# Inverting the scan's triangular blocks on TensorE by doubling, in a one-core RWKV-7 layer

## The chip, the cores and the metric

The kernel runs on one core of a Trainium2 chip. The metric is the device time in microseconds (us) of one execution of the whole program. Engines are written as in the profile: PE is TensorE (PEld its weight loads), DVE is VectorE, ACT is ScalarE, POOL is GpSimd, and SP is the engine whose queue issues the DMAs.

## The reference, cut to what matters

One inference step of a transformer-like layer: a SwiGLU feed-forward block, a token mixer, a second feed-forward block, on 128 context tokens and 1024 latent tokens with 1024 channels. The change is inside the token mixer, whose scan is the recurrence below, for 8 heads of size 64 and in both directions.

```
def step(S, inp):
    r_t, w_t, k_t, v_t, kk_t, a_t = inp
    sa = jnp.einsum('bhij,bhj->bhi', S, -kk_t)
    S = (S * w_t[:, :, None, :]
         + sa[..., None] * (kk_t * a_t)[:, :, None, :]
         + v_t[..., None] * k_t[:, :, None, :])
    return S, jnp.einsum('bhij,bhj->bhi', S, r_t)
```

The kernel computes the recurrence by chunks of 64 tokens. Inside a chunk, the vectors `sa` of the 64 tokens depend on each other through a strictly triangular 64x64 matrix N, so that the chunk needs the inverse of the unit triangular matrix I - N. A chunk's inverse does not depend on the state; only its use does.

## The kernel before

The program has three phases: feed-forward 1, the token mixer, feed-forward 2. In the mixer, the scan is cut into 18 items (`items`): two groups of four heads times eight pairs of chunks, and two context items. An item covers two chunks of four heads in each direction: 16 triangular 64x64 matrices with 32 diagonal 32x32 blocks. A direction's tile has 128 partitions (two heads, two blocks of 32 rows) and 4 matrices side by side.

For each item, three pieces of code run:

- `front` calls `stage_b` once per direction. It loads `ops` (a single buffer, 768 KB) from DRAM, makes decays and scaled operands on DVE and ACT (`fl`, `bk`, `e`), forms the raw matrices on PE (`scr`), masks them on DVE into `TT` (tile `ab`), and transposes `bk` (`bkt`). Lines L960 to L1000.
- `solve` turns the triangular matrices in `TT` into their inverses. Lines L1018 to L1089. The diagonal 32x32 blocks are copied by ACT (L995), written to DRAM (`nd`, L996) and read back with one whole block per partition (`un`, L1023; each block on four partitions). There DVE substitutes row by row: a multiply (L1036) and a sum over the last axis (L1037) for each of 7 + 2 x 3 steps, 26 instructions. The result goes through DRAM again (`xdd`, four writes L1047, two reads L1055 and L1056) back to the 32x32 layout. PE transposes it (`trx`, 24 matmuls of 32x32, L1064 and L1069), and two products of 16 matmuls each (`l64`, `l64b`, L1079 and L1084) join two 32x32 inverses to one 64x64 inverse.
- `seq_latent` or `seq_ctx` calls `step` twice. It is the state-dependent chain, in four rounds of small matmuls (`sq`, `yp`, L1121 to L1142) with copies by ACT and DVE between them.

Beside the scan, PE works off `filler`: the dense projections of the mixer (`pj`, three matmuls of 128x384 for each block, L705 to L707), and side jobs (`stage_k`, `stage_v`, `finish`; tiles `cps`, `kkb`, `bon`, `vt`, `gm`, `gv`) that need their own DMAs. A scheduler sets the order on every engine from priorities and its own cost estimates: the scan chain has the highest priority (`chain`, offset 40000), the side jobs come next, and the filler takes the places left. Each engine then runs its order strictly in sequence, so one late operand holds up everything behind it. SP's queue is in order too.

All matmuls of the scan are in fp32; the trace shows two records for each of them (L1079 issues 16 per item and 18 items give 576 records).

Of the kernel before, what the change touches and what calls it, by code (L numbers as in the profile page):

```python
# [31 lines left out]
C_ID, C_BO, C_MF, C_MB, C_SM, C_SEL, C_ONE, C_E, C_N = 0, 128, 256, 384, 512, 772, 774, 776, 856  # L32


def constants():
    c = np.zeros((128, C_N), np.float32)
    c[:, C_ID:C_ID + 128] = np.eye(128)
    hd = np.arange(128) // 64
    c[:, C_BO:C_BO + 128] = hd[:, None] == hd[None, :]
    s = np.arange(64)  # L40
    for col, keep in ((C_MF, lambda a, b: (a < b, a <= b)), (C_MB, lambda a, b: (a > b, a >= b))):
        strict, incl = keep(s[:, None], s[None, :])
        m = np.concatenate([strict, incl], 1)
        c[:, col:col + 128] = np.concatenate([m, m], 0)
# [6 lines left out]
    unit = np.zeros((32, 4, 10, 8), np.float32)  # L51
    unit[:, :, :8] = np.eye(8)
    for rep in range(4):
        for cc in range(2):
            unit[:, rep, 8 + cc, 2 * rep + cc] = 1
    c[:, C_E:C_E + 80] = unit.reshape(128, 80)
    return c
# [3 lines left out]
def body(ctx: ExitStack, tc: tile.TileContext, I: dict, y_prompt, y_sample, new_state):  # L61
# [16 lines left out]
    def pd(name="pd"):  # L78
        """a PSUM bank for a dense product, in the phases without the scan"""
# [8 lines left out]
    # ---------------------------------------------------------------- constants  # L88
# [9 lines left out]
    unit = cst[:, C_E:C_E + 80]  # L98
# [37 lines left out]
    # ---------------------------------------------------------------- pieces  # L136
# [22 lines left out]
    class Beside:  # L159
        """small products, issued after the dense products traced so far"""  # L160
# [14 lines left out]
    class Later:  # L175
        """work beside the dense products, each piece of it so many of them after the one before"""
# [98 lines left out]
    def postnorm(t, O, ssum, gp, spill, want_sum, xpool, sp):  # L275
        """x += gate * rms(O), in place of O; with want_sum the scale of the next norm."""
# [102 lines left out]
    # ---------------------------------------------------------------- FFN  # L379
# [68 lines left out]
    # ================================================================ FFN 1  # L448
    with ExitStack() as ph:
# [4 lines left out]
        def x_third(t, xp, PE, gap):  # L454
            """a third of the tokens by channels, and the scale of its norm"""
# [123 lines left out]
    # ================================================================ token mixer  # L579
# [3 lines left out]
    # ================================================================ FFN 2  # L583
    with ExitStack() as ph:
# [7 lines left out]
        def rows_of(name, tag, src, k, eng):  # L592
            """a channel block of the last third by tokens"""
# [59 lines left out]
def mixer(nc, tc, pool, env):  # L653
# [7 lines left out]
    unit = e.unit  # L661
# [6 lines left out]
    # derived per-channel parameters  # L668
# [9 lines left out]
    # per half of the partitions: the factors of b~ and k~ in the order of its rows  # L678
# [16 lines left out]
    nd = [dram.tile([2, 16, 1024], F32, name=f"nd{i}") for i in range(NI)]  # L695
    xdd = [dram.tile([2, 16, 1024], F32, name=f"xdd{i}") for i in range(NI)]
# [23 lines left out]
    def mirrored(p, row, sign, t0, n):  # L720
        """a row of the operands of a pair, and for the second head the row after or before it"""
# [24 lines left out]
    with ExitStack() as ph:  # L746
# [8 lines left out]
        YS = st.tile([128, 256], F32, name="ys")  # L755
# [4 lines left out]
        for t_ in UB + [YS]:  # L760
            G.memset(t_, 0.0)
# [106 lines left out]
        def shifted(t, d):  # L868
            """(column, source token, count) of the tokens of a third that have a neighbour."""
# [57 lines left out]
        def stage_v(p, t0, n, zv):  # L927
            """V by tokens, of a pair of heads and a block of tokens"""
# [19 lines left out]
        def zi(g, b):  # L948
            """the place of V and of the outputs of a quarter of the latents"""
            return b if g == 0 else (1, 0, 3, 2)[b]  # L950

        def stage_b(g, d, t0, A, it):
            """operands of a direction for the two chunks of tokens t0.., of two pairs of heads"""
# [51 lines left out]
        def ap_(t_, off, dims):  # L1005
            return bass.AP(tensor=t_.tensor, offset=t_.offset + off, ap=[list(t_.ap[0])] + [list(x) for x in dims])

        def diag(t_, d, s0, nb):
            """the blocks of a direction, partition by partition of the rows of a chunk"""
            return bass.AP(tensor=t_.tensor, offset=t_.offset + (d * 16 + s0 * 4) * 1024, ap=[[32, 128], [4096, nb], [1, 32]])  # L1010

        def every4(t_, r, n):
            """the partitions 4 v + r of a tile, first n columns"""
            ps = t_.ap[0][0]
            return bass.AP(tensor=t_.tensor, offset=t_.offset + r * ps, ap=[[4 * ps, 32], [1, n]])

        def solve(A, it):
# [4 lines left out]
            un = sc.tile([128, 1152], F32, name="un", tag="un")  # L1022
            SP.dma_start(un[:, 0:1024], bass.AP(tensor=nd[it].tensor, offset=nd[it].offset, ap=[[1024, 32], [0, 4], [1, 1024]]))  # L1023
            Lm = sc.tile([128, 1024], F32, name="lm", tag="lm")
            V.tensor_copy(Lm[0:64].rearrange("p (i j) -> p j i", j=32), un[0:64, 0:1024].rearrange("p (a b) -> p a b", b=32))
            S.activation(out=Lm[64:128], in_=un[64:128, 0:1024], func=AF.Copy)
            V.memset(ap_(Lm, 0, [(33, 32)]), 1.0)
            X8 = sc.tile([128, 320], F32, name="x8", tag="x8")
            S.activation(out=X8.rearrange("p (b x) -> p b x", b=4), in_=unit.unsqueeze(1).to_broadcast([128, 4, 80]), func=AF.Copy)
            tb = sc.tile([128, 4, 4, 32], F32, name="tb", tag="tb")  # L1030
            RR = tb[:, 0].rearrange("p s c -> p (s c)")[:, 0:48]

            def dot(out, a, b, dims):
                n = int(np.prod(dims))
                pv = ap_(un, 0, [(n // int(np.prod(dims[:k + 1])), dims[k]) for k in range(3)])
                V.tensor_tensor(out=pv, in0=a, in1=b, op=ALU.mult)  # L1036
                V.tensor_reduce(out=out, in_=pv, axis=AX.X, op=ALU.add)  # L1037
# [3 lines left out]
            V.tensor_copy(ap_(YS, 0, [(72, 4), (32, 2), (1, 8)]), ap_(X8, 64, [(80, 4), (8, 2), (1, 8)]))  # L1041
            for B in range(1, 4):
                n, w = 2 * B, 8 * B
                dot(ap_(RR, 0, [(8, n), (1, 8)]), ap_(Lm, 32 * w, [(0, n), (32, 8), (1, w)]), ap_(YS, 0, [(32, n), (0, 8), (1, w)]), (n, 8, w))
                dot(ap_(YS, w, [(32, n), (1, 8)]), ap_(X8, 80 * B, [(0, n), (1, 8), (8, 8)]), ap_(RR, 0, [(8, n), (0, 8), (1, 8)]), (n, 8, 8))
            for r in range(4):
                SP.dma_start(xdd[it].rearrange("d u (b r x) -> (d u) b r x", b=4, r=4)[:, :, r],  # L1047
                                         every4(YS, r, 256).rearrange("p (b x) -> p b x", b=4))
            T0, T1 = A["T"]

            def blk(t_, h, r, c):
                return t_[quad(h, r), :, 32 * c:32 * c + 32]
# [422 lines left out]
```

## Time and profile before

| what | value |
|---|---|
| median of 3 runs | 3307.19 us (3301.38, 3307.19, 3314.62) |
| profiled execution, first to last instruction (span) | 3303.1 us |
| profiled execution, own time | 3314.62 us, 11.5 us around the span |
| PE busy | 3036.7 us, 92% |
| DVE busy | 1914.0 us, 58% |
| ACT busy | 1201.1 us, 36% |
| POOL busy | 395.3 us, 12% |

The profiled execution is taken to be the longest of the three runs, since its span is longer than the shortest run and some time lies around every span. Busy time is the union of an engine's instructions. The mixer's scan lies at about 1100 to 2215 us of the span; in the feed-forward phases before and behind it nearly every slice of PE is in its highest tenth. PEclk is the clock granted to TensorE as a share of 2.4 GHz; it takes only two values, 1.0 and 0.5, so a mean of 0.89 says that 22% of a stretch ran at 1.2 GHz.

### The profile page before, as it was taken

The numbers are of one execution on the slowest core, as the hardware profiler recorded it, in microseconds if no ns is written. First come the engines' busy times: TensorE is split into PE (matmuls) and PEld (weight loads), VectorE is DVE, ScalarE is ACT, GpSimd is POOL, SyncE is SP. The second block draws the span as 40 slices with busy tenths as digits, with TensorE's granted clock in tenths as the row PEclk, the third lists the DMA queues.
The fourth block names the chain that finished last, engine by engine and source line by source line (L and its number), as shares of the span: only waits on it lengthen the run. The fifth ranks groups of instructions, "written<-read, shape, count | busy, mean of one in ns | idle before, by whom it ended". The sixth has DMA issues, their size and how long they took to land.

```text
span 3303.1 us, 54285 instructions
## 1 busy us (share of the span) xinstructions
PE 3036.7 (92%) x20956; PEld 2850.3 (86%) x20956; DVE 1914.0 (58%) x4282; ACT 1201.1 (36%) x2726; POOL 395.3 (12%) x327
## 2 busy tenths in 40 slices
PE   8999999999989677788888889899989999999998
PEld 5999999999978566677767777779989999999998
DVE  7535665556962244577877778856683233323356
ACT  5521111114546133355535456432454211121244
POOL 1000000001240111122323122100120000000012
PEclk9999999999999788799988899999999999999999
DMA  8423333225445242323333333345632111111244
GB/s 268 144 63 94 96 110 90 83 78 164 151 116 190 80 121 72 111 84 106 99 88 102 108 106 105 103 124 155 190 109 87 38 45 40 45 40 41 83 144 131
DMA packets 521742, 347.25 MB, mean 105 GB/s; under 512 B 76096, under 2 KB 497292, under 8 KB 521484
## 3 DMA queue, kind: packets, MB, share of 16 engines
q1 hardware_dynamic: 520856, 343.31, 35.2%
q8 instruction: 164, 2.69, 0.3%
q14 instruction: 94, 0.77, 0.1%
q10 hardware_dynamic: 308, 0.44, 0.0%
q0 software_dynamic: 320, 0.04, 0.0%
HBM read 277.37 MB, written 66.32 MB: 104 GB/s over the span
## 4 chain that ended last, share of the span: by engine, by line
PE 67%; DVE 16%; DMA 10%; ACT 3%; issue 2%; SPq 1%; POOL 0%; DVEq 0%; ACTq 0%; POOLq 0%
PE po L211 6%; PE po L210 6%; PE po L212 6%; PE pg L211 5%; PE pg L212 5%; PE pg L210 5%; PE pu L211 5%; PE pu L210 5%; PE pu L212 5%; PE pj L705 3%; PE pj L707 3%; PE pj L706 3%; DMA ops<-opd 3%; DMA oi<-opd 2%; DVE un L1036 1%
## 5 line engine op out<-in xcount | busy, mean ns | idle before, releaser
L138 ACT ACTIVATE whi<-wst 128x512 fp32r<-128x512 f32 (+1 forms) x578 | 353.1, 612 | 792.7 <-PE po L212 389.4
L139 DVE TENSOR_TENSOR wlo<-wst,whi 128x512 fp32r<-128x512 f32 (+1 forms) x480 | 325.2, 678 | 305.8 <-ACT whi L138 296.2
L705 PE MATMUL pj<-hh,wlo 128*128 128x384 f32 x1056 | 393.8, 373 | 4.3 <-ACT xcs L783 1.8
L706 PE MATMUL pj<-hl,whi 128*128 128x384 f32 x1056 | 393.7, 373 | 2.3 <-DVE hl L265 1.3
L707 PE MATMUL pj<-hh,whi 128*128 128x384 f32 x1056 | 391.9, 371 | 0.0
L211 PE MATMUL pg<-hl,whi 128*128 128x384 f32 x1056 | 355.9, 337 | 6.4 <-POOL hl L263 5.0
L210 PE MATMUL po<-ah,wlo 128*128 128x384 f32 x1056 | 355.4, 337 | 3.0 <-ACT ah L138 3.0
L210 PE MATMUL pg<-hh,wlo 128*128 128x384 f32 x1056 | 356.8, 338 | 1.4 <-DVE wlo L139 1.3
L211 PE MATMUL po<-al,whi 128*128 128x384 f32 x1056 | 354.8, 336 | 0.4 <-DVE al L139 0.4
L212 PE MATMUL pg<-hh,whi 128*128 128x384 f32 x1056 | 355.0, 336 | 0.0
L210 PE MATMUL pu<-hh,wlo 128*128 128x384 f32 x1056 | 355.0, 336 | 0.0
L212 PE MATMUL po<-ah,whi 128*128 128x384 f32 x1056 | 354.2, 336 | 0.0
L211 PE MATMUL pu<-hl,whi 128*128 128x384 f32 x1056 | 353.8, 335 | 0.0
L212 PE MATMUL pu<-hh,whi 128*128 128x384 f32 x1056 | 353.5, 335 | 0.0
L273 POOL TENSOR_TENSOR ss<-ss,sqt 128x384 f32<-128x384 f32 x78 | 88.5, 1138 | 1679.5 <-ACT sqt L272 1675.0
L426 DVE TENSOR_TENSOR sil<-sil,pu 128x384 f32<-128x384 f32 x132 | 72.8, 552 | 353.0 <-PE pu L212 353.0
L398 DVE TENSOR_TENSOR o<-o,po 128x384 f32<-128x384 f32 x288 | 159.2, 553 | 168.2 <-PE po L212 167.5
L705 PEld LDWEIGHTS pj<-hh,wlo 128*128 128x128 f32 x1056 | 215.6, 204 | 13.8 <-issue 2.1
L706 PEld LDWEIGHTS pj<-hl,whi 128*128 128x128 f32 x1056 | 215.9, 204 | 10.8 <-DVE hl L265 2.2
L707 PEld LDWEIGHTS pj<-hh,whi 128*128 128x128 f32 x1056 | 215.7, 204 | 7.0
L139 POOL TENSOR_TENSOR wlo<-wst,whi 128x512 fp32r<-128x512 f32 x98 | 134.6, 1376 | 622.7 <-ACT whi L138 486.1
L211 PEld LDWEIGHTS pg<-hl,whi 128*128 128x128 f32 x1056 | 199.7, 189 | 8.8 <-POOL hl L263 6.5
(621 smaller groups left out, 5848.6 us busy)
## 6 DMA issues: line engine op xcount, KB each, us to landing
wst<-in_ffn_w SPq DMA_DIRECT2D x324, 256.0 KB
wmod<-in_w_mod SPq DMA_DIRECT2D x144, 256.0 KB
ops<-opd SPq DMA_DIRECT2D x36, 768.0 KB
wst<-in_w_in SPq DMA_DIRECT2D x94, 256.0 KB
wst<-in_ffn_w SPq DMA_DIRECT2D x96, 192.0 KB
xo<-xd SPq DMA_DIRECT2D x64, 192.0 KB
wst<-in_w_out SPq DMA_DIRECT2D x48, 256.0 KB
opd<-zv SPq DMA_DIRECT2D x24, 384.0 KB
```

Source lines behind the costliest of these rows:

```text
L138: S.activation(out=hi, in_=src, func=AF.Copy)
L139: eng.tensor_tensor(out=lo, in0=src, in1=hi.bitcast(F32), op=ALU.subtract)
L210: PE.matmul(ps, lo, xh, start=(k == 0), stop=False)
L211: PE.matmul(ps, hi, xl, start=False, stop=False)
L212: later.tick(PE.matmul(ps, hi, xh, start=False, stop=(k == nk - 1)))
L273: eng.tensor_tensor(out=ssum, in0=ssum, in1=q, op=ALU.add)
L398: V.tensor_tensor(out=O[m][t], in0=O[m][t], in1=ps, op=ALU.add)
L426: V.tensor_tensor(out=s, in0=s, in1=pu, op=ALU.mult)
L705: PE.matmul(ps, lo, xh, start=(k == 0), stop=False)
L706: PE.matmul(ps, hi, xl, start=False, stop=False)
L707: ins = PE.matmul(ps, hi, xh, start=False, stop=(k == 7))
L1036: V.tensor_tensor(out=pv, in0=a, in1=b, op=ALU.mult)
```

## The change

The substitution on DVE and both trips through DRAM go. POOL now makes two tiles in `stage_b`: `U` (the triangular block plus the identity) and `X` (`U` masked to its 2x2 diagonal blocks, the first level of the inverse). `solve` transposes `U` on PE (`trx`, 32 matmuls) and then runs four levels, at each of which blocks of the inverse double in size: `xmt` (32 matmuls), a mask by DVE, `xtn` and `xn` (32 matmuls each), and a copy of `xtn` by DVE and of `xn` by ACT. The last two products (`l64`, `l64b`) stay. The 32x32 matmuls of an item go from 56 to 448. The code of `front`, `step`, the filler and the jobs stays as it was, and so do the priorities.

```
+    i, j = np.arange(32)[:, None], np.arange(32)[None, :]
+    for l in range(5):
+        pairs = (i >> l != j >> l) & (i >> l + 1 == j >> l + 1)
+        c[:, C_LM + 32 * l:C_LM + 32 * l + 32] = np.tile(pairs | (i == j), (4, 1))
...
-            N = q1.tile([128, 4, 32], F32, name="nt_", tag="nt_")[:, :nb]
-            for h in range(2):
-                for b_ in range(2):
-                    S.activation(out=N[quad(h, b_)], in_=TT[quad(h, b_), s0:s0 + nb, 32 * b_:32 * b_ + 32], func=AF.Copy)
-            SP.dma_start(diag(nd[it], d, s0, nb), N)
+            U, X = A["U"], A["X"]
+            for q in quads:
+                c = slice(q.start % 64, q.start % 64 + 32)
+                G.tensor_tensor(out=U[q, d], in0=TT[q, s0:s0 + nb, c], in1=ident[q, q].unsqueeze(1).to_broadcast([32, nb, 32]), op=ALU.add)
+            G.tensor_tensor(out=X[:, d], in0=U[:, d], in1=lmask[0].unsqueeze(1).to_broadcast([128, nb, 32]), op=ALU.mult)
...
-            SP.dma_start(un[:, 0:1024], bass.AP(tensor=nd[it].tensor, offset=nd[it].offset, ap=[[1024, 32], [0, 4], [1, 1024]]))
...
-            for m in range(1, 8):
-                dot(ap_(X8, m, [(80, 4), (8, 10)]), ap_(Lm, 32 * m, [(264, 4), (0, 10), (1, m + 1)]), ap_(X8, 0, [(80, 4), (8, 10), (1, m + 1)]), (4, 10, m + 1))
...
-            for B in range(1, 4):
...
-            for r in range(4):
-                SP.dma_start(xdd[it].rearrange("d u (b r x) -> (d u) b r x", b=4, r=4)[:, :, r],
...
+            def product(name, tag, lhsT, rhs):
+                ps = ps_.tile([128, 2, 4, 32], F32, name=name, tag=tag)
+                for d in range(2):
+                    for s in range(4):
+                        for q in quads:
+                            PE.matmul(ps[q, d, s], lhsT[q, d, s], ident[q, q] if rhs is None else rhs[q, d, s], start=True, stop=True)
+                return ps
...
+            def masked(out, ps, l):
+                V.tensor_tensor(out=flat(out), in0=flat(ps), in1=lmask[l].unsqueeze(1).to_broadcast([128, 8, 32]), op=ALU.mult)
...
+            Xt = part("xt")
+            masked(Xt, product("trx", "sc", U, None), 0)
+            for l in range(1, 5):
+                R = part("xr")
+                masked(R, product("xmt", "sc", U, Xt), l)
+                pt = product("xtn", "sq", X, R)
+                px = product("xn", "sc", R, X)
+                Xt = part("xt")
+                V.tensor_copy(Xt, pt)
+                if l < 4:
+                    X = part("xx")
+                    S.activation(out=X, in_=px, func=AF.Copy)
+                    continue
+                for d in range(2):
+                    for h in range(2):
+                        S.activation(out=blk(d, h, 1 - d, 1 - d), in_=px[quad(h, 1 - d), d], func=AF.Copy)
+                for d in range(2):
+                    for h in range(2):
+                        V.tensor_copy(blk(d, h, d, d), px[quad(h, d), d])
```

The scheduler sets a new order from this. PE before, in the fifth item's `solve`: the two transposes `trx` of the substituted blocks and the first matmul of `l64`, with projections (`pj`) between them.

```order
L706 MATMUL pj<-hl_0_8298,whi 128x384
L1064 MATMUL trx<-cst,tb 32x32 x8
L168 MATMUL cps<-cst,oi 128x2 x2
L707 MATMUL pj<-hh_0_8297,whi 128x384
L1069 MATMUL trx<-cst,tb 32x32 x16
L705 MATMUL pj<-hh_0_8326,wlo 128x384
L706 MATMUL pj<-hl_0_8327,whi 128x384
L707 MATMUL pj<-hh_0_8326,whi 128x384
L1079 MATMUL l_13210<-tb,ab_12907 32x32
L705 MATMUL pj<-hh_1_8847,wlo 128x384
L706 MATMUL pj<-hl_1_8848,whi 128x384
L707 MATMUL pj<-hh_1_8847,whi 128x384
```

Between the ends of two consecutive solves stand 113 to 205 projections (`pj`) in this order, for the third to the eighteenth item.

PE now, in the same item's `solve`: the product `xmt` of the third level, the projections behind it, and `xtn` and `xn` that use its masked result.

```order
L1016 MATMUL xmt<-sol_14591,u_14367 32x32 x32
L701 MATMUL pj<-hh_0_8266,wlo 128x384
L702 MATMUL pj<-hl_0_8267,whi 128x384
L703 MATMUL pj<-hh_0_8266,whi 128x384
L701 MATMUL pj<-hh_0_8297,wlo 128x384
L702 MATMUL pj<-hl_0_8298,whi 128x384
L703 MATMUL pj<-hh_0_8297,whi 128x384
L1016 MATMUL xtn<-sol_14591,sol_14592 32x32 x32
L1016 MATMUL xn<-sol_14592,sol_14591 32x32 x32
```

Few projections are left between the dependent products, and few in an item as a whole: 23 to 46 in ten of the 18 items, 61 to 147 in five, and 260, 309 and 566 in three; 743 follow the last solve (189 before).

DVE before, in the fifth item's `solve`: substitution steps (L1036 and L1037) with instructions of side jobs and of `step` between them.

```order
L1087 COPY ab_12388<-l64b 32x4x32
L1036 TENSOR_TENSOR un<-lm,x_13139 128x200
L225 TENSOR_TENSOR nt<-ny 128x4
L1037 TENSOR_REDUCE x_13139<-un 128x40
L226 TENSOR_TENSOR nt<-nt,nh 128x4
L1140 COPY zv_9492<-sq 64x2x64
L1036 TENSOR_TENSOR un<-lm,x_13139 128x240
L227 SCALAR_TENSOR_TENSOR ny<-nt,ny 128x4
L1140 COPY zv_9493<-sq 64x2x64
```

DVE now, in the same item's `solve`: the mask of an `xmt`, then two instructions of the next item's `stage_b` that need its load of `ops` (L972 `bk`, L959 `fl`), then the copy of `xtn`.

```order
L1030 TENSOR_TENSOR sol_14591<-xmt,cst 128x256
L972 TENSOR_TENSOR bk<-ops 128x512
L959 SCALAR_TENSOR_TENSOR fl<-cst,sg 128x260
L1043 COPY sol_14591<-xtn 128x256
L973 TENSOR_TENSOR bk<-bk,ff 128x512
L976 TENSOR_TENSOR e_15309<-ops,fl 64x4x64
L977 TENSOR_TENSOR e_15309<-ops,fl 64x4x64
```

The 26 substitution instructions of each item are gone from DVE; the copy that the next PE product needs now stands behind instructions that wait for a DMA.

## Rows read from the trace of the kernel before

**Rows 1.** The page: span, and busy time of each engine with its share.
```profile
span 3303.1 us, 54285 instructions
PE 3036.7 (92%) x20956; PEld 2850.3 (86%) x20956; DVE 1914.0 (58%) x4282; ACT 1201.1 (36%) x2726; POOL 395.3 (12%) x327
```

**Rows 2.** The page: 40 equal slices of the span, busy tenths and granted clock.
```profile
PE   8999999999989677788888889899989999999998
PEclk9999999999999788799988899999999999999999
```

**Rows 3.** Stretches: busy us (instructions) by engine, then granted clock, DMA share, GB/s.
```profile
1050.00:1230.00 180.00, 126.42 (x763) 117.82 (x761) 64.34 (x150) 55.42 (x123) 26.38 (x20) 0.83 0.36 109
1230.00:2165.00 935.00, 797.52 (x8033) 672.19 (x8029) 686.57 (x1866) 443.31 (x1207) 203.13 (x152) 0.89 0.35 100
```

**Rows 4.** The page: the chain that ended last, by engine.
```profile
PE 67%; DVE 16%; DMA 10%; ACT 3%; issue 2%; SPq 1%; POOL 0%; DVEq 0%; ACTq 0%; POOLq 0%
```

**Rows 5.** Waits of PE, 1230 to 2165 us: total us, times, longest.
```profile
PE bon L168 <- DVE od L898: 19.4, 5, 7.9
PE bkt L999 <- ACT e L990: 15.3, 8, 7.3
PE gv L171 <- DVE ysq L1179: 15.2, 10, 2.9
PE kkb L171 <- DVE oi L915: 9.1, 4, 2.8
```

**Rows 6.** Timeline of PE at full clock: start, duration, instructions.
```profile
1450.62 0.33 PE L705 MATMUL pj<-hh,wlo 128*128 128x384 f32 x1
1450.79 0.34 PE L706 MATMUL pj<-hl,whi 128*128 128x384 f32 x1
1451.06 0.44 PE L1064 MATMUL trx<-cst,tb 32*32 32x32 f32 x16
1451.43 0.44 PE L707 MATMUL pj<-hh,whi 128*128 128x384 f32 x1
1451.80 0.45 PE L1069 MATMUL trx<-cst,tb 32*32 32x32 f32 x32
1452.18 0.44 PE L705 MATMUL pj<-hh,wlo 128*128 128x384 f32 x1
```

**Rows 7.** Timeline of PE at half clock.
```profile
1231.71 0.52 PE L705 MATMUL pj<-hh,wlo 128*128 128x384 f32 x1
1232.03 0.52 PE L706 MATMUL pj<-hl,whi 128*128 128x384 f32 x1
```

**Rows 8.** Tile `un` alone, 1230 to 2165 us: busy on DVE, then ACT.
```profile
1230.00:2165.00 935.00, 252.57 (x459) 17.95 (x17) 0.89 0.35 100
```

**Rows 9.** Groups, 1230 to 2165 us: busy us, mean ns, idle before.
```profile
L1079 PE MATMUL l<-tb,ab 32*32 32x32 f32 x576 | 12.2, 199 | 1.1 <-DVE tb L1071 0.5 <-ACT tb L1070 0.4
L906 DVE TENSOR_TENSOR or<-or,bon 128x256 f32<-128x256 f32 x11 | 4.6, 418 | 1.3 <-PE bon L168 1.2
L1130 ACT ACTIVATE rz<-sq 128x256 f32<-128x256 f32 x34 | 13.0, 382 | 22.4 <-PE sq L1121 20.3 <-PE yp L1133 1.7
L991 POOL TENSOR_TENSOR e<-e,cst 64x512 f32<-64x512 f32 x64 | 89.7, 1402 | 261.2 <-ACT e L990 232.4 <-issue 13.4 <-ACT nt__16702 L995 12.8
```

**Rows 10.** Waits of DVE, 1230 to 2165 us.
```profile
DVE od L895 <- DMA oi<-opd: 55.3, 12, 16.2
DVE bk L977 <- DMA ops<-opd: 26.6, 13, 7.3
```

**Rows 11.** Timeline of DVE: `stage_b` around two loads of `ops`.
```profile
1524.30 0.42 DVE L982 TENSOR_TENSOR e<-ops,ff 64x256 f32<-64x256 f32 x1
...
1530.00 1.19 DVE L977 TENSOR_TENSOR bk<-ops 128x512 f32<-128x512 f32 x1 [0.69 <-DMA ops<-opd]
...
1535.77 0.42 DVE L982 TENSOR_TENSOR e<-ops,fl 64x256 f32<-64x256 f32 x1
...
1545.13 0.69 DVE L977 TENSOR_TENSOR bk<-ops 128x512 f32<-128x512 f32 x1 [1.39 <-DMA ops<-opd]
```

More of the change, by code (lines that the diff above doesn't have):

```diff
@@ L30 @@
 SEGS = [[(0, 128, 0), (128, 384, 1)], [(0, 384, 1)], [(0, 384, 1)]]
-C_ID, C_BO, C_MF, C_MB, C_SM, C_SEL, C_ONE, C_E, C_N = 0, 128, 256, 384, 512, 772, 774, 776, 856
+C_ID, C_BO, C_MF, C_MB, C_SM, C_SEL, C_ONE, C_LM, C_N = 0, 128, 256, 384, 512, 772, 774, 776, 936
 def constants():
@@ L50, in constants @@
     c[:, C_ONE] = 1
[L51 to L56, printed above, removed]
+    i, j = np.arange(32)[:, None], np.arange(32)[None, :]
+    for l in range(5):
+        pairs = (i >> l != j >> l) & (i >> l + 1 == j >> l + 1)
+        c[:, C_LM + 32 * l:C_LM + 32 * l + 32] = np.tile(pairs | (i == j), (4, 1))
     return c
@@ L97, in body @@
     ones = cst[:, C_ONE:C_ONE + 1]
-    unit = cst[:, C_E:C_E + 80]
+    lmask = [cst[:, C_LM + 32 * l:C_LM + 32 * l + 32] for l in range(5)]
     par = per.tile([128, 128 + 100], F32, name="par")
@@ L660, in mixer @@
     ident, bones, masks, smask, sel, ones, per = e.ident, e.bones, e.masks, e.smask, e.sel, e.ones, e.per
-    unit = e.unit
+    lmask = e.lmask
     after, PB, later = e.after, e.PB, e.later
@@ L694, in mixer @@
     NI = 18
-    nd = [dram.tile([2, 16, 1024], F32, name=f"nd{i}") for i in range(NI)]
-    xdd = [dram.tile([2, 16, 1024], F32, name=f"xdd{i}") for i in range(NI)]
     def proj(col, evac, ts=range(NT)):
@@ L754, in mixer @@
         SG = st.tile([128, 4, 65], F32, name="sg")
-        YS = st.tile([128, 256], F32, name="ys")
         YL = st.tile([128, 4, 2, 256], F32, name="yl")
@@ L759, in mixer @@
         G.memset(SG[:, :, 0:1], 0.0)
-        for t_ in UB + [YS]:
+        for t_ in UB:
             G.memset(t_, 0.0)
@@ L1003, in quad @@
             return slice(64 * h + 32 * b, 64 * h + 32 * b + 32)
[L1005 to L1015, printed above, removed]
@@ new lines, in mixer, with solve, flat, part @@
+        quads = [quad(h, b) for b in range(2) for h in range(2)]
+        def solve(A):
+            U, X = A["U"], A["X"]
+            T = A["T"]
+            def product(name, tag, lhsT, rhs):
[5 more added lines that the diff above has]
+                return ps
+            def flat(t_):
+                return t_.rearrange("p d s c -> p (d s) c")
+            work = [sc.tile([128, 4, 2, 4, 32], F32, name=f"sol{i}", tag=("un", "lm")[i]) for i in range(2)]
+            turn = {"xt": [work[0][:, 0], work[0][:, 1]], "xr": [work[0][:, 2], work[0][:, 3]], "xx": [work[1][:, 0], work[1][:, 1]]}
+            def part(name):
+                turn[name].reverse()
+                return turn[name][0]
+            def masked(out, ps, l):
+                V.tensor_tensor(out=flat(out), in0=flat(ps), in1=lmask[l].unsqueeze(1).to_broadcast([128, 8, 32]), op=ALU.mult)
+            def blk(d, h, r, c):
+                return T[d][quad(h, r), :, 32 * c:32 * c + 32]
+            Xt = part("xt")
[17 more added lines that the diff above has]
+                        V.tensor_copy(blk(d, h, d, d), px[quad(h, d), d])
+            order = [(d, h, d, 1 - d) for d in range(2) for h in range(2)]
@@ L1075, in solve @@
             ps = ps_.tile([128, 4, 32], F32, name="l64", tag="sq")
-            order = [(d, h, d, 1 - d) for d in range(2) for h in range(2)]
             for s in range(4):
                 for d, h, b0, b1 in order:
-                    PE.matmul(ps[quad(h, b1), s], blk(A["T"][d], h, b0, b1)[:, s], TB[d][quad(h, b0), s], start=True, stop=True)
-            S.activation(out=PB, in_=ps, func=AF.Copy)
-            ps2 = ps_.tile([128, 4, 32], F32, name="l64b", tag="sq")
+                    PE.matmul(ps[quad(h, b1), s], blk(d, h, b0, b1)[:, s], Xt[quad(h, b0), d, s], start=True, stop=True)
@@ L1082, in solve @@
+            R = part("xr")[:, 0]
+            S.activation(out=R, in_=ps, func=AF.Copy)
+            ps = ps_.tile([128, 4, 32], F32, name="l64b", tag="sq")
             for s in range(4):
                 for d, h, b0, b1 in order:
-                    PE.matmul(ps2[quad(h, b0), s], PB[quad(h, b1), s], D0[quad(h, b1), s] if d == 0 else blk(T1, h, b1, b1)[:, s], start=True, stop=True)
+                    PE.matmul(ps[quad(h, b0), s], R[quad(h, b1), s], blk(d, h, b1, b1)[:, s], start=True, stop=True)
@@ L1085, in solve @@
             for d, h, b0, b1 in order:
                 if h:
-                    V.tensor_copy(blk(A["T"][d], h, b0, b1), ps2[quad(h, b0)])
+                    V.tensor_copy(blk(d, h, b0, b1), ps[quad(h, b0)])
                 else:
-                    S.activation(out=blk(A["T"][d], h, b0, b1), in_=ps2[quad(h, b0)], func=AF.Copy)
+                    S.activation(out=blk(d, h, b0, b1), in_=ps[quad(h, b0)], func=AF.Copy)
         def group(products):
@@ L1158, in item_bufs @@
             ab = [s2.tile([128, 2, 4, 128], F32, name=f"ab{d}", tag=f"AB{d}") for d in range(2)]
-            return {"T": [t_[:, 0] for t_ in ab], "BT": [t_[:, 1] for t_ in ab],
+            return {"U": s2.tile([128, 2, 4, 32], F32, name="u32", tag="U"), "X": s2.tile([128, 2, 4, 32], F32, name="x32", tag="X"),
+                    "T": [t_[:, 0] for t_ in ab], "BT": [t_[:, 1] for t_ in ab],
                     "FT": [s2.tile([128, 4], F32, name=f"ft{d}", tag=f"FT{d}") for d in range(2)],
@@ L1361, in mixer @@
             front(0)
-            solve(A[0], 0)
+            solve(A[0])
         for i, (g, j) in enumerate(items):
@@ L1381, in mixer @@
                 if i + 1 < NI:
-                    solve(A[i + 1], i + 1)
+                    solve(A[i + 1])
             if i == 0:
```

44 lines of the change are left out of this document (removed).

## The prediction

> **What bounds the kernel now.** I read the page first. PE is busy for 3036.7 of the 3303.1 us, DVE for 58% [rows 1], and the chain that ended last runs for 67% over PE [rows 4]. The slices show one place where PE is not full: the fourteenth to the twenty-sixth, which is the scan of the token mixer, and there its clock sinks too [rows 2]. So the next view was the busy time by stretch. From 1050 to 1230 us, before the first `solve` gives its result, PE idles for 180.0 - 126.4 = 53.6 us; from 1230 to 2165 us for 935.0 - 797.5 = 137.5 us, at a mean granted clock of 0.89 [rows 3]. Since the clock has only the levels 1.2 and 2.4 GHz, 22% of the 935 us, 206 us, ran at the lower one.
>
> Then the waits of PE in that stretch. The largest are side jobs that find DVE or ACT late (`bon`, `gv`, `kkb`, `bkt`), not the scan's `solve` [rows 5]. PE runs one order, the dense projections stand in it, and their number is fixed. So the stretch ends when PE has done all its work, plus its idle time. DVE, with 687 busy us of 935, makes PE late here and there but does not set the end. What the change does to the time is therefore: PE work added, less idle time removed, plus idle time made.
>
> **PE work added.** A 32x32 fp32 matmul shows as two records. Sixteen of them take 0.45 us from the first start to the last end, and one record lasts 0.199 us, so they start (0.45 - 0.199)/31 = 8.1 ns apart [rows 6, 9]. A run of them among projections costs a little at either end: the projection ahead takes 0.27 us to the next start instead of 0.17, and 0.38 us pass from the run's start to the next projection, 0.12 more than 32 records of 8.1 ns [rows 6]. That is 0.22 us for a run.
>
> An item has 448 such matmuls after the change, 896 records: 896 x 8.1 ns = 7.3 us, and about 8 separate runs add 1.8 us, together 9.0. Before, 56 matmuls took 112 x 8.1 ns = 0.9 us, the first 16 records 0.1 us more (they start 16 ns apart, since only two quarters of the array are used), and four or five runs 1.0 us, together 2.0. The difference of 7.0 us, 18 times, is 126 us at full clock. At half clock a projection takes 0.32 us where it takes 0.17 at the full one [rows 6, 7]; if the added work met the low clock for 22% of its time, it would be 126 x 1.2 = 151 us. I take 138, the middle, because the new order puts 743 of the projections behind the last solve, where PE runs undisturbed at full clock now, and the solves into the rest. Bounds: 114 us (784 records, no run ends), and 296 us (all at 16 ns, (784 x 16 ns + 1.2 us) x 18 = 247, and 1.2 for the clock).
>
> [...]
>
> **Idle time removed.** From DVE go the 26 substitution instructions and the copy ahead of them: 253 us on the tile `un` [rows 8]. It gets 5 masks and 4 copies of 128x256 from PSUM at 0.42 us [rows 9], 3.8 us, and 4 small copies, in all under 5 us an item, 90 us. ACT loses the `lm` and `un` work, 18 us, and the copies to and from the DRAM layout, and gets 3 copies of 0.38 us [rows 9]. SP loses 162 issues (36 `nd`, 18 `un`, 72 `xdd`, 36 `tb`), each of which held up the loads behind it while it waited. So the waits of PE for late DVE work should shrink: `bon`, `gv` and `kkb` are 43.7 us [rows 5]. With a few for `xdd` itself I take 50 us off; between 0 and 137.5 is possible. What stays is every wait for the side jobs' own loads (DVE waits 55.3 us for `oi` alone [rows 10]) and the 53.6 us before the first solve, which the change does not touch.
>
> **Idle time made.** A solve is now ten dependent rounds of product, evacuation, product, all of them in PE's order. Where DVE is free, a mask of 0.42 us is covered by the four to seven projections behind the product (0.7 to 1.2 us), a copy of `xtn` by `xn`. It isn't always free. The new order puts `bk` and `fl` of the next `stage_b` between a mask and the copy that PE needs, and both wait for the load of `ops`. That tile has one buffer: its last reader ended at 1524.72 and `bk` of the next load began at 1530.00, 5.3 us later; the next time it was 1536.19 to 1545.13, 8.9 us [rows 11]. Two loads an item, and 6.2 us from `bk` to the last reader between them, make a loop of 23 to 30 us an item. Before, an item had 797.5/17 = 47 us of PE work and the loop was slack. In the ten items with only 23 to 46 projections it has about 100 fewer of them, so 47 - 21 + 7 = 33 us, and the slack is nearly gone. I take 2.2 us of PE idle for each of the two loads.
>
> POOL gets eight small additions and two masks an item. No row shows their size: the 64x512 one takes 1.40 us [rows 9], a quarter of the columns is between 0.35 and 1.40. I take 0.4, 4 us an item, 72 in all, beside POOL's 203 us in the stretch. They stand between the last `scr` and `trx`, where about 2 us of PE work covers them; 1.1 us an item is left. That makes 5.5 us in each of the ten sparse items, 55 us. Bounds: 0 (everything covered) and 14 us an item, 140 us (the whole latency of both loads).
>
> **The sum.** 138 - 50 + 55 = +143 us. The profiled execution took 3314.6 us, so it would take 3458. The median of the three runs lies 7.4 us lower: 3450.
>
> **Rivals.**
> - *The scan chain becomes the bound* (slower still). Place: DVE's copy of `xtn` behind `bk` and `fl`. From 5.5 us of waits a sparse item on, it decides. With 8 us more in each of the ten items the time is 3450 + 80 = 3530. For it: the 8.9 us of rows 11 and the waits for `ops` in rows 10. Against it: with the `nd`, `un` and `xdd` traffic gone the loads may land sooner. [...]
> - *The idle time goes* (faster). One mechanism: DVE no longer late, PE never waits long, and the clock stays high. There are 137.5 us of idle time and at most 103 us lost to the low clock (half of 206) to be had, 240 together; it decides from 138 us on. At three quarters, 180 us, the time would be 3307 + 138 - 180 = 3265. For it: DVE loses 253 us, and PE waits for DVE. Against it: the largest waits hang on DMAs of side jobs, and a denser chain of small products makes new ones.
> - *The products start 16 ns apart*, as `trx` before, not 8.1. Then 247 us more at full clock, some 270 at the mean one, and about 3570. Against it: the loops walk all four quarters, as the run of 32 records does [rows 6].
> - *What goes and what comes are equal*, about 3307: the removed waits would have to be near 138 us.
>
> **How the numbers follow.** What a measurement can tell from no change is about 0.5%, 16 us. Forecast 0.60 (its own range 3400 to 3500), scan chain 0.18, faster 0.12, 16 ns 0.04, equal 0.06. So faster 0.12, same 0.06, slower 0.82. A range from 3310 to 3550 leaves out the faster case, the 16 ns case and half of the equal one, 0.19; the idle bounds (0 to 137.5 off, 0 to 140 on) reach to both of its ends.
>
> **What would show it.** Right: PE's busy time in the scan larger by about 140 us; runs of 64 records about 0.7 us long; DVE's busy time smaller by some 160 us; no wait named `nd`, `un` or `xdd`; PE waiting for the masks and the copies of `xtn` in the items with few projections; idle time of the scan still above 100 us. The working is wrong if PE's busy time grows by much less than 114 us, if the idle time from the first solve to the end of the scan falls below 40 us, or if `xtn` waits more than 10 us an item.

## The result, and the profile after

The changed kernel takes 3628.7 us (median of four runs, 3624.1 to 3634.7) beside 3304.3 us before (3300.6 to 3314.6): 1.0968 times as long, 95% interval 1.0939 to 1.0996 (the two medians alone give 1.098). The prediction had slower, 3450 us, with a range up to 3550. The direction was right; of the 324 us the sum held 143. The profiled execution of the changed kernel took 3627.5 us, 1.8 more than its span, and in all runs below the two lie 1.7 to 2.2 us apart; so the profiled execution before was not the one of 3314.6 us, 11.5 above its span, that the table and the prediction take it for. The forecast does not hang on this: it is the median before plus 143.

The page of the changed kernel: span, busy time, two rows of the 40 slices, the DMA queue of the instructions (packets, MB, share) and the chain that ended last.

```profile
span 3625.7 us, 82046 instructions
PE 3275.7 (90%) x35068; PEld 3088.9 (85%) x35068; DVE 1730.0 (48%) x3940; ACT 1136.4 (31%) x2546; POOL 466.7 (13%) x506
...
PE   8999999999886778786788887989998999999998
...
PEclk9999999999997867777778788989999999999999
...
q8 instruction: 275, 4.51, 0.5%
...
PE 70%; DMA 10%; DVE 9%; issue 7%; ACT 2%; POOL 1%; SPq 1%; ACTq 0%; DVEq 0%; POOLq 0%
```

Beside [rows 1], DVE lost 184 us (some 160 were foretold), and PE gained 239. Beside [rows 2], the slices below nine tenths of the clock reach from the thirteenth to the twenty-seventh; before, from the fourteenth to the twenty-third. In the chain, "issue" (the engine waits for nothing that the profile shows) grew from 2% [rows 4] to 7%. The queue that carries instructions moved 164 packets before:

```profile
q8 instruction: 164, 2.69, 0.3%
```

The same two stretches as in [rows 3], the second longer by the 322 us that the span grew:

```profile
1050.00:1230.00 180.00, 122.16 (x1601) 110.55 (x1600) 56.43 (x153) 50.74 (x115) 31.73 (x38) 0.80 0.31 97
1230.00:2487.00 1257.00, 1032.22 (x21354) 896.07 (x21354) 545.79 (x1651) 395.18 (x1072) 263.16 (x311) 0.80 0.22 66
```

So the whole loss lies here. PE's busy time rose from 126.4 + 797.5 = 923.9 to 1154.4 us, by 230; its idle time from 191.1 to 282.6 us, by 92. The time at the lower clock, worked out as in the prediction, went from 267 us (0.34 of 180 and 0.22 of 935) to 575 (0.40 of both stretches). The clock records of both traces hold the shares 1.0 and 0.5 alone, 38 records of each before and 57 of each after. Matmuls of 128x384 one behind the other start 173 ns apart at the full share and 320 ns at the half one, medians in both traces. 384 columns in 320 ns are 1.2 a ns: from that the 1.2 GHz of the lower clock, and 2.4 at twice the share, are estimates (384 in 173 ns are 2.2).

Waits of PE from 1230 to 2487 us, beside [rows 5]:

```profile
PE xmt L1016 <- issue: 40.6, 24, 3.6
PE bon L166 <- DVE od L893: 37.8, 6, 9.8
PE xn L1016 <- issue: 22.1, 19, 3.4
PE xmt L1016 <- DVE sol L1043: 15.1, 8, 9.0
PE xtn L1016 <- issue: 14.8, 14, 3.1
...
PE trx L1016 <- POOL u L990: 5.5, 12, 0.9
```

A new kind of wait leads the list: 77.5 us before `xmt`, `xn` and `xtn` whose releaser is "issue", that is, PE waited for nothing that the profile shows. The timeline shows where they stand (start, duration, instructions; in brackets the idle time before). At full clock and then, from 1870.6 us on, at half:

```profile
1864.74 0.76 PE L1016 MATMUL xmt<-sol,u 32*32 32x32 f32 x63
...
1870.02 0.74 PE L1016 MATMUL xn<-sol,sol 32*32 32x32 f32 x62
1870.72 0.31 PE L1016 MATMUL xmt<-sol,u 32*32 32x32 f32 x2
1872.35 1.07 PE L1016 MATMUL xmt<-sol,u 32*32 32x32 f32 x62 [1.31 <-issue]
```

A run of 64 records does take 0.7 us at full clock, as foretold. But PE stops for 1.31 us after the second record of an `xmt`, between two matmuls of one product with the same operands. The profile names no mask, copy or load that was late there. Over the scan there are 65 such stops, 89.6 us in all, 59 of them (79.6 us) in the middle of an `xmt`, `xtn` or `xn`; before there was none. The rest of the idle time, 193 us, is what it was (191). (`trx` stops in its middle too, 12 times for 5.5 us, but there the profile names POOL's `u`.)

The places of the stops tell more than their length. Count PE's instructions as the trace lists them (weight loads, matmuls and those of its sequencer) from the first one on, in blocks of 256: the matmul behind each of the 65 stops is the 194th or 195th instruction of its block, whatever product is cut. Of PE's 128 other stops of more than 0.15 us, 2 stand there. In the kernels below that have such stops they have the same place: with these 65, 317 of 319 in ten traces, and the other two are one instruction beside it. The instruction queue keeps the same step in the changed kernel's trace: its 275 packets are 16384 bytes each and take 1.0 us at the median, PE's 70467 instructions are 275 blocks of 256 (before, 164 packets and 42182 instructions), and each of the 65 stops ends 1.2 to 1.6 us after one of the packets has landed.

Two durations that the prediction estimated, 1230 to 2487 us:

```profile
L990 POOL TENSOR_TENSOR u<-ab,cst 32x128 f32<-32x128 f32 x128 | 61.3, 479 | 340.8 <-DVE ab L984 329.1 <-PE cps L166 3.6 <-DVE nt L224 3.3
...
L1030 DVE TENSOR_TENSOR sol<-xmt,cst 128x256 f32<-128x256 f32 x68 | 28.7, 422 | 87.4 <-PE xmt L1016 87.1
```

POOL's small addition takes 0.48 us (0.4 was taken), the mask 0.42, as taken. One operation that the change does not touch grew: the 576 `scr` of the scan, before and after.

```profile
L988 PE MATMUL scr<-e,bk 64*128 64x128 f32 x576 | 71.9, 307 | 18.3 <-DVE bk L978 10.7 <-DVE e L982 6.3 <-ACT zv L1128 1.4
L983 PE MATMUL scr<-e,bk 64*128 64x128 f32 x576 | 106.1, 381 | 37.1 <-DVE bk L973 20.1 <-DVE e L977 8.2 <-ACT e L985 5.5
```

Of these records 64% start at the lower clock, 15% before.

### The profile page after: what moved, and what is told of

Read it like the earlier page. It is cut to its first block, busy times and chain, and to the rows that moved or that the text cites. A ratio compares the mean times of both kernels' runs of the same rounds, so it can differ in the third digit from the quotient of the medians.

```text
span 3625.7 us, 82046 instructions
## 1 busy us (share of the span) xinstructions
PE 3275.7 (90%) x35068; PEld 3088.9 (85%) x35068; DVE 1730.0 (48%) x3940; ACT 1136.4 (31%) x2546; POOL 466.7 (13%) x506
## 3 DMA queue, kind: packets, MB, share of 16 engines
q8 instruction: 275, 4.51, 0.5%
## 4 chain that ended last, share of the span: by engine, by line
PE 70%; DMA 10%; DVE 9%; issue 7%; ACT 2%; POOL 1%; SPq 1%; ACTq 0%; DVEq 0%; POOLq 0%
PE po L209 5%; PE po L208 5%; PE po L210 5%; PE pg L209 5%; PE pg L210 5%; PE pg L208 5%; PE pu L209 5%; PE pu L208 5%; PE pu L210 5%; PE pj L703 3%; PE pj L701 3%; PE pj L702 3%; DMA oi<-opd 3%; DMA opd<-oi 3%; PE scr L983 2%
```

## The experiments

Three theories for the 181 us that the sum did not hold. **I, supply of instructions:** a 32x32 fp32 matmul is two weight loads and two matmul instructions: the PE and PEld counts grew by 28224, 4 for each of 18 x 392 matmuls. The instruction queue grew by 111 packets, 254 instructions a packet. If such a block comes only so often, a long run of tiny matmuls uses its instructions up. **W, work:** the small products simply cost more than 8.1 ns a record, wherever they stand. **D, dependent rounds:** product, mask, product, copy is a chain that stretches the scan. "Stalls" below are PE's idle times in the scan whose releaser is "issue", added up from the records (none before, 90 us in the changed kernel; the 85 us of the expectations take in the 5.5 us of `trx` that wait for POOL, and leave out a few stops elsewhere). "Low-clock time" is that of the scan, by the clock records (259 us before, 567 in the changed kernel). Each kernel but q_space16_r3 was timed once; seven runs of the kernel before, in one session, lie between 3296.6 and 3317.9 us.

**a_repeat.** The kernel before, with its second transpose repeated so that each item has 392 more 32x32 matmuls, and nothing else changed:

```diff
+            for rep in range(24):
+                for s in range(4):
+                    for h in range(2):
+                        for b_ in (1, 0):
+                            q = quad(h, b_)
+                            PE.matmul(ps[q, 1, s], TB[1][q, s], ident[q, q], start=True, stop=True)
...
```

> The kernel before, with its second transpose of each item issued 24 and a half times over into the same PSUM columns: 392 more 32x32 matmuls an item, as many as the change adds, with no new dependency, mask, copy or POOL work. If only the array's work counts (W), it costs 126 us at full clock to 190 us at the rate measured in the changed kernel: 3430 to 3490. If the supply of instructions counts (I: the new stalls fall in the middle of products, and 110 more blocks of 16 KB of instructions are fetched), the run of 416 matmuls outruns its supply too, with stalls of 0.5 to 3 us inside it: 85 to 250 us on top, 3520 to 3700. If the dependent rounds make the idle time (D), there are no stalls inside the run and the time is W's.

Measured: 3679.2 us, 372 more than before (3307.5) in the same session. This kernel has no doubling, no masks and all of the old substitution, and loses more than the changed kernel. Its timeline in one item's run, and its largest wait of PE (the whole scan):

```profile
1604.56 2.33 PE L1070 MATMUL trx<-cst,tb 32*32 32x32 f32 x161
1608.34 1.92 PE L1070 MATMUL trx<-cst,tb 32*32 32x32 f32 x128 [1.46 <-issue]
1611.81 1.93 PE L1070 MATMUL trx<-cst,tb 32*32 32x32 f32 x128 [1.55 <-issue]
1615.29 1.93 PE L1070 MATMUL trx<-cst,tb 32*32 32x32 f32 x128 [1.54 <-issue]
1619.58 1.93 PE L1070 MATMUL trx<-cst,tb 32*32 32x32 f32 x128 [2.36 <-issue]
1623.05 1.00 PE L1070 MATMUL trx<-cst,tb 32*32 32x32 f32 x58 [1.54 <-issue]
```

```profile
PE trx L1070 <- issue: 171.0, 89, 4.2
```

The stops come exactly every 128 records, that is 256 instructions with the weight loads, and three of the four periods are 3.47 or 3.48 us: 27 ns a record in a long run, not 8.1. This stretch ran at the lower clock (the projections behind it start 0.32 us apart), where the 128 records alone take 1.93 us. Two blocks of the same kernel in another item, the first of them at full clock throughout with its stop behind it, show that the period is not the clock's doing:

```profile
1965.44 1.28 PE L1070 MATMUL trx<-cst,tb 32*32 32x32 f32 x128 [0.44 <-issue]
1968.91 1.39 PE L1070 MATMUL trx<-cst,tb 32*32 32x32 f32 x128 [2.19 <-issue]
```

The records take 1.28 us there, the stop behind them 2.19, and the period is 3.47 us again. The instruction queue of this kernel moved what the changed kernel's did, 275 packets, 4.51 MB: 111 packets of 16 KB more than before, 4.51 - 2.69 MB. The stops are 1.46 to 2.36 us at each of the first five block ends shown.

**c_s2 and c_s1.** The changed kernel with two, and with one, of the four matrices in each product (the others are left out): the ten rounds, the masks, the copies (narrower, as the products are) and POOL's work stay, the instructions of the products are halved and quartered.

```diff
-                    for s in range(4):
+                    for s in range(2):
                         for q in quads:
```

> The changed kernel with two of the four matrices in each product (half of the blocks are left out, so the inverses of the others are not made): the same ten dependent rounds, evacuations half as wide, 448 matmuls become 240. W: half of the 195 us of product work goes, about 3530. I: that, and more than half of the 85 us of stalls inside products, and part of the time at the low clock: 3420 to 3480. D: rounds unchanged, about 3600.

> The same with one of the four matrices: 448 matmuls become 136, the ten rounds stay. W: 140 us less than the changed kernel, about 3490. I: that and all the stalls inside products, 3330 to 3400, at or little above the kernel before. D: about 3600.

Measured: 3442.0 and 3361.5 us, the ranges of I. Stalls 18 us and none, low-clock time 441 and 362 us. In c_s1 `trx` still stops in its middle, but for POOL. Its wait and its stretches:

```profile
PE trx L1016 <- POOL u L990: 12.5, 17, 2.2
```

```profile
1050.00:1230.00 180.00, 133.25 (x1188) 118.29 (x1186) 58.34 (x162) 55.66 (x134) 32.37 (x38) 0.80 0.31 96
1230.00:2221.00 991.00, 868.03 (x10550) 727.82 (x10545) 510.89 (x1643) 374.79 (x1054) 271.09 (x310) 0.85 0.28 83
```

With all rounds in place PE idles 46.8 + 123.0 = 169.7 us, 21 less than before the change. The longest contiguous runs of small matmuls are 192 records in the changed kernel, 96 in c_s2 and 46 in c_s1. The rounds are not what costs; D falls.

**h_lv34.** The same question from the other side: full products, fewer rounds (levels 1 and 2 of the doubling are left out).

```diff
-            for l in range(1, 5):
+            for l in range(3, 5):
```

> The changed kernel with levels 3 and 4 of the doubling alone (levels 1 and 2 are left out): 7 rounds of products instead of 13, 224 small matmuls of products an item, beside c_s2's 208 in all 13 rounds (3441.95 us). Supply of instructions (I): the count decides and the contiguous runs are as long as in the changed kernel, 3420 to 3480, instruction DMA about 220 packets, stalls inside products 25 to 45 us. Dependent rounds (D): six rounds fewer than c_s2 at some 1.5 us each in 18 items, about 160 us under it where nothing covers them, 3280 to 3350.

Measured: 3446.5 us, stalls 25 us. With 7 products in place of 13 and nearly c_s2's count of matmuls, the time is c_s2's within 5 us. The count decides, the rounds don't.

**p_low.** The whole computation, with `solve` taken out of the chain's priority, so that the scheduler leaves 112 to 128 projections in most items:

```diff
-                if i + 1 < NI:
-                    solve(A[i + 1])
+            if i + 1 < NI:
+                solve(A[i + 1])
             if i == 0:
```

> The changed kernel, whole computation, with solve traced outside the scan chain's priority, so that its products stand among 112 to 128 projections an item instead of 23 to 46. W: the number of instructions is the same, so no gain beyond covered rounds: 3560 to 3640. I: between products the supply catches up, so stalls inside products go from 85 us to under 30, and the clock stays higher: 3420 to 3500. D: rounds are covered by projections: idle time falls by the 40 us that wait for masks, copies and ops, 3580.

Measured: 3597.3 us; my expectation under I was missed, and the time lies in W's range. Stalls stayed at 90 us, for the most part before `xmt`:

```profile
PE xmt L1016 <- issue: 49.3, 26, 3.1
```

The projections moved between the items, but the products still stood in contiguous runs of up to 96 matmuls (`xtn`, `xn`, the next `xmt`). I had taken the number of projections in an item for the spacing of the products. What counts is what lies inside a run.

**q_space16 and q_space8.** So the order inside the run was set by hand: same computation, same instructions, but in 13 solves each 16 matmuls are followed by a block of three projections (in 12 solves each 8, for q_space8), taken from the fill behind the item.

```diff
-                            PE.matmul(ps[q, d, s], lhsT[q, d, s], ident[q, q] if rhs is None else rhs[q, d, s], start=True, stop=True)
+                            ins = PE.matmul(ps[q, d, s], lhsT[q, d, s], ident[q, q] if rhs is None else rhs[q, d, s], start=True, stop=True)
+                            if prev is not None:
+                                after(ins, prev)
+                        if nsol[0] in range(2, 15) and 4 * d + s in (3, 7):
...
+                            prev = next(filler, None)
...
-            fill(GI)
+            fill(16 if 1 <= i < 14 else GI)
```

> The changed kernel, whole computation and same instructions, but in 13 of the 18 solves each piece of 16 small matmuls is followed by one block of three projections, by order alone (the projections are taken from the fill behind the item). Supply (I): 64 small-matmul instructions in some 0.7 us are still above one fetch block of 256 per 3.5 us only in bursts, so stalls inside products fall from 85 us to under 35, half-clock time of the scan from 567 to under 430, and the time to 3480 to 3560. Products cost what they cost wherever they stand (W): 3610 to 3640. Dependent rounds (D): each round is stretched by the projections put into it, so the chain gets longer, 42 blocks of about 0.5 us an item, 3700 and more.

> As q_space16 with pieces of 8 in 12 solves (four blocks of projections a product, which uses up the projections that else follow the last solve). Supply (I): stalls inside products of those solves gone, under 25 us in all, 3450 to 3540. W: 3610 to 3640. D: 3800 and more.

Measured: q_space16 3564.1 us, 65 less than the changed kernel and 4 above the range that I gave; W had 3610 and more. Timed again, four runs beside the kernel before:

> q_space16 again, timed in three rounds: 1.074 to 1.083 of the kernel before, where the changed kernel is at 1.0968 [1.0939, 1.0996]; if the one look was chance, 1.09 and more.

Measured: 3575.6 us, 53 less than the changed kernel; 1.0816 times the kernel before, 95% interval 1.0781 to 1.0850, which lies clear of the changed kernel's 1.0939 to 1.0996. The profile of q_space16: the pieces in the timeline, its "issue" waits of products in the scan, and its stretches.

```profile
1816.84 0.45 PE L1030 MATMUL xn<-sol,sol 32*32 32x32 f32 x32
1817.22 0.44 PE L702 MATMUL pj<-hh,wlo 128*128 128x384 f32 x1
1817.50 0.34 PE L705 MATMUL pj<-hl,whi 128*128 128x384 f32 x1
1817.67 0.35 PE L706 MATMUL pj<-hh,whi 128*128 128x384 f32 x1
...
1818.48 0.45 PE L1030 MATMUL xmt<-sol,u 32*32 32x32 f32 x32
```

```profile
PE xn L1030 <- issue: 6.0, 6, 1.8
PE xmt L1030 <- issue: 3.0, 3, 2.0
PE xtn L1030 <- issue: 2.4, 3, 1.2
```

```profile
1050.00:1230.00 180.00, 125.94 (x1712) 114.50 (x1711) 57.83 (x162) 49.69 (x113) 29.24 (x36) 0.73 0.31 95
1230.00:2424.00 1194.00, 1032.67 (x21253) 842.83 (x21254) 538.57 (x1625) 389.18 (x1058) 263.82 (x312) 0.87 0.23 68
```

Order alone took the stalls from 90 us to 14 (11.4 of them in these lines) and PE's idle time from 282.6 to 54.1 + 161.3 = 215.4, by 67; PE's busy time is the same (1158.6 for 1154.4), though the low-clock time fell from 567 to 396 us. So the 64 us of the span are idle time, and the stalls fell by 76.

q_space8 was a miss, 3740.5 us, and neither W nor D explains it. Its stalls are down to 22.8 us, but PE's busy time is 3409.2 us, 133.5 more than in the changed kernel. It has 689 ends of runs of `trx`, `xmt`, `xtn` and `xn`, the changed kernel 277. At the 0.22 us a run that the prediction took from [rows 6], 412 more are 91 us; the records, from one start to the next, show 75 us more on `pj` and 35 on the products. Cutting a run has its price here, 110 us for 412 ends, and pieces of 8 are past the point where it pays.

**r_bf16 and s_both.** The operands in bfloat16 (which leaves out precision) make one weight load and one matmul instruction of each product (15466 matmul records in the scan for the changed kernel's 22955, some 18 x 416 fewer), with the same products and rounds; s_both puts them into q_space16's order.

```diff
-            return {"U": s2.tile([128, 2, 4, 32], F32, name="u32", tag="U"), "X": s2.tile([128, 2, 4, 32], F32, name="x32", tag="X"),
+            return {"U": s2.tile([128, 2, 4, 32], BF16, name="u32", tag="U"), "X": s2.tile([128, 2, 4, 32], BF16, name="x32", tag="X"),
```

> The changed kernel with the operands of the solve's products in bfloat16, which leaves out precision: one weight load and one matmul instruction for each product instead of two of each, same products, same rounds, same masks. Supply (I): instruction DMA about 217 packets and a time as c_s2's, which has as many instructions at half the products, 3400 to 3480; stalls inside products under 30. Products (W): half the records at 14 ns each, but no stall goes, 3520 to 3550. Dependent rounds (D): 3600 to 3630.

> q_space16's order with r_bf16's operands (which leaves out precision): both halve what comes too fast. Supply (I): no stall inside a product that counts (under 8 us), the scan's half-clock time under 400 us, 3400 to 3440. If the spacing costs by itself what it saves once stalls are few, 3455 to 3480.

Measured: r_bf16 3460.4 us with stalls of 7 us, in the range of I. Its low-clock time is 492 us all the same. With c_s2 it makes a pair: half the products in fp32, or all of them in one pass, and both move the same number of instruction packets:

```profile
q8 instruction: 216, 3.54, 0.4%
```

The times lie 18 us apart. s_both took 3522.0 us, above both of its ranges. Its stalls are down to 0.7 us, but it has 190 more ends of runs than r_bf16, 42 us at 0.22 us each; PE's busy time is 44 us longer, and its idle time 17. That makes the 61 us. With few stalls left to save, the spacing only costs.

**n_none.** The changed kernel without any product of the doubling (joins kept), to price the gain alone:

```diff
-            Xt = part("xt")
-            masked(Xt, product("trx", "sc", U, None), 0)
-            for l in range(1, 5):
...
+            Xt = X
```

> The changed kernel without any product of the doubling (the inverse of the diagonal blocks is left out, the joins to 64 stay): no substitution on VectorE, no gather, no small products. It prices the gain by itself. By the prediction's step 'idle removed' (50 us of waits for bon, gv and kkb behind VectorE) 3240 to 3270; if those waits are only put in another place, 3290 to 3310.

Measured: 3278.9 us, 30 less than before (3308.5), between the two expectations and 18 below the fastest of the seven runs. Its stretches, its waits of PE and the wait behind `bon`, beside [rows 10]:

```profile
1050.00:1230.00 180.00, 126.13 (x1014) 111.99 (x1012) 58.67 (x162) 61.75 (x149) 31.64 (x38) 0.84 0.33 101
1230.00:2139.00 909.00, 750.59 (x6975) 659.16 (x6976) 502.11 (x1480) 365.40 (x984) 265.10 (x310) 0.88 0.30 89
```

```profile
PE scr L983 <- DVE e L977: 31.9, 9, 14.2
PE bon L166 <- DVE od L893: 30.5, 5, 9.7
...
DVE od L890 <- DMA oi<-opd: 75.9, 14, 13.9
```

PE idles 53.9 + 158.4 = 212.3 us, 21 more than before, with the substitution gone. The gain is all in PE's busy time, 923.9 to 876.7 us. Of these 47 us the transposes and joins of the old solve are 15; what makes the rest was not settled. Over the whole execution, `pj` takes 34 us less (662 for 697, from one start to the next).

No version that keeps any products of the doubling beats the kernel before, and n_none says why none was sought further: with the inverse for nothing the gain is 30 us, and even a quarter of the products, in c_s1, costs 83 us more than that.

## Why the prediction was wrong, step by step

- **What bounds the kernel:** right. The scan ends when PE has done its work plus its idle time; 230 us more work and 92 us more idle time are the 322 us.
- **PE work added** is the step that failed, in its size and in what it left out. It priced 784 records an item at 8.1 ns from a run of 32 [rows 6], which is shorter than one block of 256 instructions. The products, joins included, took 195 us more, not 138 (228.5 for 33.9). Two things were too small in it: about 40% of the records, not 22%, met the lower clock, where starts inside a run came some 14 ns apart on average (stops left out) against 9 at the full one; and the solves have 277 run ends, 15 an item, not 8. The upper bound of 296 us, from 16 ns a record, did hold this part.
- **What it left out:** the stalls, 90 us. They are no operation and no wait on another engine, and the kernel before has none. The instruction counts from which they could be suspected were at hand: 392 more matmuls an item are 1568 more instructions, with long runs among them. And the other work of PE grew by about 36 us (230 - 195). That is a net figure, since 140 fewer of the `pj` matmuls lie in the stretch; `scr` alone takes 34 us more, with 64% of its records at the lower clock for 15%.
- **Idle time removed** (50 us) was wrong: n_none shows 21 us more idle time without the substitution, and `bon`, the largest wait of [rows 5] at 19.4 us, is at 30.5. DVE waits 75.9 us for `oi` in n_none, 55.3 before [rows 10]: the waits hung on the side jobs' own loads, as the prediction said against its "faster" rival, not on how much DVE had to do.
- **Idle time made** (55 us) was wrong as well: in the changed kernel `xmt` waits 15.1 us for the copies of `xtn` (in the fifth item DVE idles 0.94 us before `bk`, the copy two places behind it) and `trx` 5.5 us for POOL, and c_s1 has all the rounds with less idle time than before. That the two errors cancel is luck: 50 off and 55 on were 5 together; measured, without the stalls, 2.
- **The rivals.** The scan chain was given 0.18, with 3530 us; c_s1 and h_lv34 show that it does not decide. The products 16 ns apart, 0.04, came nearest to the time with 3570, but not by its mechanism: half of the starts inside a run are 7 ns apart or less, at either clock. A long run goes at 27 ns a record (a_repeat) as an average over quick blocks and stops. That the first `trx` before starts its records 16 ns apart because it uses only two quarters of the array was an estimate: at full clock the starts of L1064, on two quarters, are 16.7 ns apart on average and those of L1069, on four, 8.6 (pauses of 150 ns and more left out), but no run varied the quarters alone.
- **What would show it:** the signs that held (runs of 0.7 us, DVE's 184 us, no `nd`, `un` or `xdd`) told of the operations. The one on PE's busy time failed: 230 us more for about 140; the sign of being wrong beside it looked only at the other side, growth much under 114 us. None asked whether PE would wait for nothing.

The sum, by its terms: 138 - 50 + 55 = 143 became 194.6 (products) + 35.9 (other work, `scr` above all) + 89.6 (stalls) + 1.9 (all other idle time) = 322. That the stalls come from the supply of instructions is shown by their places, every one at the same place of a block of 256 instructions and 1.2 to 1.6 us behind a landed packet, by a_repeat, which makes them without the change, and by q_space16, which removes most of them (90 us to 14) by order alone. What lowers the clock was not isolated. The low-clock time fell with the number of instructions (c_s1, c_s2) and with the spacing (q_space16), in which both the stops and the runs of small products change; but r_bf16 has hardly a stop and 492 us of it, so the stops alone do not make it.

## What to carry to other kernels

Count the instructions, not only the time of each: when tiny matmuls replace a few large operations, compare the longest contiguous run of them with the block at whose ends PE stopped (here 256 instructions, 3.47 us in a_repeat), and price the run beyond it by that, not by the spacing of a short one (8.1 ns). Shorter runs are not quite safe: with 96 records, 192 instructions, c_s2 still stalled for 18 us; with at most 46, c_s1 did not. An engine that stops between two identical instructions, with "issue" as releaser, may be waiting for instructions: see whether its stops keep one place in a block of instructions, as 65 of 65 did here in blocks of 256. Three projections behind each 16 matmuls took the stalls from 90 us to 14 (q_space16), at an estimated 0.22 us [rows 6] to 0.27 us (110 us for 412 ends, q_space8) for each cut. And before working out a gain, ask what the time would be with the new part for nothing: here it was 30 us, less than any version of the new part costs.

## What the runs showed of the hardware that I had not expected

- A contiguous stream of 32x32 fp32 matmuls goes at 128 records in 3.47 us, 27 ns each, at the lower as at the full clock (a_repeat), while 32 of them in a row start 8.1 ns apart [rows 6].
- A wait inside a `solve` can be followed by slower work. In the changed kernel an `xmt` waited 9.0 us for a copy of `xtn`; PE was busy for 3.73 of 10 us, and the products behind it ran at the lower clock (granted share 0.50) through the next two stretches of 10 us. This is one place; no run shows that the wait made the clock fall. The wait, then the stretches (columns as in [rows 3]):

```profile
1803.09 1.08 PE L1016 MATMUL xmt<-sol,u 32*32 32x32 f32 x64 [9.00 <-DVE sol L1043]
```

```profile
1780.00:1790.00 10.00, 10.00 (x120) 8.22 (x120) 7.44 (x43) 3.94 (x13) 0.00 (x0) 1.00 0.32 97
1790.00:1800.00 10.00, 3.73 (x105) 2.87 (x103) 0.25 (x2) 1.95 (x7) 0.00 (x0) 0.95 0.19 60
1800.00:1810.00 10.00, 6.68 (x264) 5.78 (x265) 3.49 (x9) 1.40 (x3) 0.00 (x0) 0.50 0.14 44
1810.00:1820.00 10.00, 8.13 (x293) 6.98 (x293) 4.79 (x27) 1.01 (x2) 1.27 (x1) 0.50 0.13 36
```
